# An MLP with fast matrix multiplication: the sums of one weight tile made two periods later, and its store put behind those of six other tiles

## The chip, the cores and the metric

One core of a Trainium2 chip. The metric is the device time of one execution in microseconds (us). "PE" is the tensor engine, "VectorE" (DVE), "ScalarE" (ACT) and "GpSimd" (POOL) are the other engines, and "SP" is the sync engine, which here only issues DMAs.

## The reference, cut to what matters

```python
# x: 16 x 512 x 768, w1: 768 x 3072, b1: 3072, w2: 3072 x 768, all float32
y = np.matmul(x, w1) + b1
y = 0.5 * y * (1.0 + erf(y / np.sqrt(2.0)))          # GELU
return np.matmul(y, w2).astype(np.float32)
```

## The kernel before

Both products use a scheme with seven instead of eight block products (p1 to p7). It needs sums of blocks: of x (`x_sums`), and of each tile of W1 (`prep_wt`: four VectorE subtractions of 128x384). W1 has 12 tiles; a finished tile, with its sums, is also stored to a scratch tensor in HBM (`keep`), from which the later stages load it. In the early stage, which the change touches, the kernel works on two blocks of x ("0" and "1") in a hand-written order of units. Unit (0, k) or (1, k) is W1 tile k with x block 0 or 1.

```python
seq = ([(0, k) for k in range(7)] +
       [(1, 0), (1, 1), (1, 2), (0, 7), (1, 3), (0, 8), (1, 4), (0, 9), (1, 6), ...])
at = {u: n for n, u in enumerate(seq)}          # at[1, 0] == 7, at[1, 1] == 8

def prep_wt(n):                                 # four sums, put in a list; run when sums() pops them
    o = {s: w1_op(wts[n], s) for s in range(7)}
    for d, a, b in ((T3, B22, T1), (T1, T1, B11), (T2, B22, T1), (T4, B21, T2)):
        later(KQ * P, lambda d=d, a=a, b=b: tt(o[d], o[a], o[b], SUB), soon)

def keep(n):
    nc.sync.dma_start(out=w1s[hi_of(n)][:], in_=wts[n])
```

A period works on the new unit i and finishes the previous unit j. Each `fill(slot)` is a place where VectorE sums and DMA issues are put between the parts. bX, bY, bZ and bW are the buffers that PE's products go to, "arena" is the kernel's working memory on the chip, and c22 and c12 are two blocks of the result, each finished by one VectorE add:

```python
p1(i); copy_xy(i)        # PE -> bX;  ScalarE copies bX to bY
p7(j)                    # PE -> bY;  VectorE: c22 add (reads bY)         L608 (in add_c22)
fill(1)
p5(i)                    # PE -> bW;  ScalarE copy
fill(2)
p3(j)                    # PE -> bZ;  VectorE: c12 add                    L636
fill(3)
p6(i)                    # PE -> bY;  VectorE: copy bZ<-bY (even units)   L654
j.right_done()           # ScalarE: GELU, needs both adds of j            L399
fill(4)
p4(j); fill(5)           # PE accumulates into bY of j; ScalarE: GELU     L404
p2(i); fill(6)           # PE -> bX;  ScalarE: GELU                       L404
```

And the part of the early stage's `fill` that is changed (`loads_a` issues the loads of x and of W1 tiles; tile 7 goes into tile 0's buffer, tile 8 into tile 1's):

```python
def fill_a(pos, slot):
    # ... cut ...
    if slot == (1 if pos < at[1, 0] else 4) and pos + 1 < len(seq) and seq[pos + 1][0] == 0:
        prep_wt(seq[pos + 1][1])                # the next unit's tile
    if slot == 4:
        if pos in (3, 4):
            prep_wt(pos - 3)                    # tiles 0 and 1, wanted only from pos 7 and 8 on
    # ... cut ...
    if slot == 1:
        if pos in (at[1, 0] - 2, at[1, 0] - 1): # pos 5 and 6
            h = pos - at[1, 0] + 2
            x_sums(1, soon, slice(h * RH // 2, (h + 1) * RH // 2))
    # ... cut: sums() pops some of the list in slots 1, 2, 4 and 5 ...
    if slot == 5:
        loads_a(pos)
        if pos < 5:
            transposes_a(pos)                   # DMA transposes of x block 1, on SP
        if seq[pos][0] == 1:
            keep(seq[pos][1])                   # stores in the order 0, 1, 2, 3, 4, 6, 5, ...
    if slot == 6:
        flush(soon)
```

## Time and profile before

| | before |
|---|---|
| median of the first 3 runs | 854.24 us (853.19 to 854.71) |
| span of the profile | 852.4 us |
| PE, VectorE, ScalarE busy | 99%, 78%, 49% |
| PE clock | full |

The first line of the profile's page that matters gives the busy time of each engine:

```profile
PE 845.8 (99%) x6432; PEld 569.2 (67%) x6432; DVE 667.8 (78%) x1128; ACT 421.1 (49%) x686; POOL 83.3 (10%) x135
```

A change in the early stage can only win by closing a gap on PE. The timeline of PE in the kernel before, around the place of the change (start, duration, engine, line, operation, then in brackets the idle time before it and what ended it), shows one:

```profile
40.59 0.81 PE L383 MATMUL bZ<-arena 128*128 128x512 f16 x3
41.78 1.46 PE L383 MATMUL bY<-arena 128*128 128x512 f16 x6 [0.38 <-ACT bY L601]
43.08 1.46 PE L383 MATMUL bX<-arena 128*128 128x512 f16 x6
44.39 0.81 PE L383 MATMUL bY<-arena 128*128 128x512 f16 x3
...
46.40 1.46 PE L383 MATMUL bY<-arena 128*128 128x512 f16 x6
47.70 1.46 PE L383 MATMUL bX<-arena 128*128 128x512 f16 x6
```

Read starts, not durations: three matmuls at 40.59 should be followed at 41.24, and the next start at 41.78, so 0.54 us are lost (the bracket says 0.38, because it counts from a modelled end). The six bY matmuls at 46.40 are p6 of one unit and p4 of the unit before it; the bX group follows 1.30 us later, so nothing is lost there.

The chain of waits of the kernel before, over the same stretch, says what the gap at 41.78 hangs on:

```profile
24.64 11.81 DMA arena<-in_w_dram
...
36.47 0.37 DVE arena L189
...
37.61 0.61 DVE arena L636
...
38.24 1.15 ACT arena L399
...
41.13 0.61 ACT bY L601
...
41.78 1.46 PE bY L383 x6
```

W1 tile 6 lands at 36.44 us. Three of its sums come next on VectorE, the c12 add stands behind them, ScalarE's GELU waits for that add, and the copy bY<-bX, which PE needs, stands behind the GELU.

The timeline of VectorE in the kernel before shows the place from which tile 1's sums are taken (four of the five at 33.76) and the place to which they go (behind the last two x sums at 44.24, ahead of the c22 add at 45.30):

```profile
33.76 1.79 DVE L189 TENSOR_TENSOR arena<-arena 128x384 f16<-128x384 f16 x5
35.47 0.68 DVE L608 TENSOR_TENSOR arena<-bY,arena 128x512 f32<-128x512 f32 x1
36.47 1.14 DVE L189 TENSOR_TENSOR arena<-arena 128x384 f16<-128x384 f16 x3 [0.32 <-DMA arena<-in_w_dram]
...
44.24 1.02 DVE L189 TENSOR_TENSOR arena<-arena 128x768 f16<-128x768 f16 x2
45.30 0.69 DVE L608 TENSOR_TENSOR arena<-bY,arena 128x512 f32<-128x512 f32 x1
```

### The profile page before, as it was taken

The page shows a single profiled execution, that of the slowest core. Times are in us where ns is not written, and L with a number is a line of the kernel's source. Part 1 is how long each engine was busy: PE and PEld are TensorE (multiplying, and loading weights), DVE is VectorE, ACT ScalarE, POOL GpSimd, SP SyncE. Part 2 cuts the span into 40 slices and gives each one's busy share as a digit, 9 for nine tenths or more (in the row PEclk, how much of TensorE's full clock was granted, in tenths as well). Part 3 has the DMA queues.
Part 4 walks back from the last instruction along what each step waited for, and adds up shares of the span by engine and source line. Part 5 has one row for each costly group of instructions (what it writes and reads, how often), then busy time and mean ns, then how long its engine had stood idle before and what let it go on. Part 6 is the DMA issues. An engine that isn't in the chain of part 4 may idle for free.

```text
span 852.4 us, 16481 instructions
## 1 busy us (share of the span) xinstructions
PE 845.8 (99%) x6432; PEld 569.2 (67%) x6432; DVE 667.8 (78%) x1128; ACT 421.1 (49%) x686; POOL 83.3 (10%) x135
## 2 busy tenths in 40 slices
PE   9999999999999999999999999999999999999998
PEld 5444445687544897448974499645995469944798
DVE  4956678786657998679976799667996689956998
ACT  4777762122277513774138722477216771267611
POOL 5021100002100002000020000200012000010000
PEclk9999999999999999999999999999999999999999
DMA  9995987649989698996989789896998969967398
GB/s 225 201 271 86 256 166 257 253 190 221 227 242 290 206 326 289 294 265 228 337 285 298 220 279 335 278 300 192 312 343 257 311 177 329 354 218 270 99 310 284
DMA packets 143522, 219.05 MB, mean 257 GB/s; under 512 B 61756, under 2 KB 84724, under 8 KB 143444
## 3 DMA queue, kind: packets, MB, share of 16 engines
q1 hardware_dynamic: 117968, 179.83, 66.0%
q0 software_dynamic: 25440, 38.15, 20.9%
q8 instruction: 50, 0.82, 0.4%
q14 instruction: 28, 0.23, 0.1%
q10 hardware_dynamic: 36, 0.01, 0.0%
HBM read 180.30 MB, written 47.87 MB: 268 GB/s over the span
## 4 chain that ended last, share of the span: by engine, by line
PE 93%; DMA 5%; ACT 1%; DVE 0%; issue 0%; POOL 0%; ACTq 0%
PE bY L383 20%; PE bY L488 15%; PE bX L383 13%; PE bX L488 10%; PE bZ L383 7%; PE bW L383 7%; PE bZ L488 5%; PE bW L488 5%; PE bY L427 5%; DMA arena<-in_x_dram 3%; PE bZ L427 2%; PE bW L427 2%; PE bX L427 2%; DMA arena<-in_w_dram 1%; DMA arena<-w1s 1%; PE bY L575 1%
## 5 line engine op out<-in xcount | busy, mean ns | idle before, releaser
L189 DVE TENSOR_TENSOR arena<-arena 128x1536 f16<-128x1536 f16 (+7 forms) x632 | 403.5, 669 | 6.0 <-PE bW L427 1.1
L383 PEld LDWEIGHTS <-arena 128*128 128x128 f16 x1974 | 192.4, 98 | 225.7 <-DMA arena<-w1s 1.8
L488 PEld LDWEIGHTS <-arena 128*128 128x128 f16 x3528 | 292.1, 98 | 8.4 <-issue 0.4
L383 PE MATMUL bY<-arena 128*128 128x512 f16 x846 | 214.4, 379 | 0.4 <-ACT bY L601 0.4
L608 DVE TENSOR_TENSOR arena<-bY,arena 128x512 f32<-128x512 f32 (+1 forms) x102 | 69.4, 681 | 126.7 <-PE bY L383 88.2
L383 PE MATMUL bX<-arena 128*128 128x512 f16 x564 | 138.6, 379 | 0.6 <-DMA arena<-w1s 0.5
L488 PE MATMUL bY<-arena 128*128 128x192 f16 x1500 | 138.3, 246 | 0.0
L601 ACT COPY bY<-bX 128x512 f32<-128x512 f32 (+1 forms) x143 | 78.6, 550 | 119.4 <-DVE arena L537 82.0
L399 ACT ACTIVATE arena<-arena,b1t 128x1024 f16<-128x1024 f32 x94 | 108.0, 1149 | 54.0 <-DVE arena L636 54.0
L621 ACT COPY arena<-bW 128x512 f32<-128x512 f32 (+1 forms) x147 | 81.0, 551 | 92.0 <-PE bW L488 43.9
L488 PE MATMUL bX<-arena 128*128 128x192 f16 x1020 | 93.1, 246 | 0.1
L636 DVE TENSOR_TENSOR arena<-bZ,arena 128x512 f32<-128x512 f32 (+1 forms) x102 | 69.3, 679 | 22.7 <-PE bZ L383 18.7
L383 PE MATMUL bZ<-arena 128*128 128x512 f16 x282 | 76.2, 379 | 0.0
L383 PE MATMUL bW<-arena 128*128 128x512 f16 x282 | 76.2, 379 | 0.0
L427 PEld LDWEIGHTS <-arena 128*128 128x128 f16 x528 | 51.6, 98 | 34.1 <-issue 0.2
L404 ACT ACTIVATE arena<-bX,b1t 128x512 f16<-128x512 f32 x94 | 64.0, 681 | 10.0 <-PE bX L383 10.0
L520 POOL DMA_DIRECT2D out_dram<-arena x42 | 30.5, 728 | 391.8 <-DVE arena L632 355.6
L404 ACT ACTIVATE arena<-bY,b1t 128x512 f16<-128x512 f32 x94 | 63.3, 674 | 0.0
L652 ACT COPY bZ<-bY 128x512 f32<-128x512 f32 (+1 forms) x54 | 29.0, 537 | 66.0 <-DVE arena L636 31.8
L294 POOL DMA_DIRECT2D arena<-in_x_dram x60 | 32.3, 544 | 265.0 <-DMA arena<-arena 154.6
L488 PE MATMUL bZ<-arena 128*128 128x192 f16 x504 | 48.5, 246 | 0.0
L488 PE MATMUL bW<-arena 128*128 128x192 f16 x504 | 48.5, 246 | 0.0
(60 smaller groups left out, 401.2 us busy)
## 6 DMA issues: line engine op xcount, KB each, us to landing
arena<-w2s SPq DMA_DIRECT2D x294, 288.0 KB, 4.6
arena<-w1s SPq DMA_DIRECT2D x72, 672.0 KB, 6.5
out_dram<-arena POOLq DMA_DIRECT2D x42, 384.0 KB, 4.7
w2s<-arena SPq DMA_DIRECT2D x49, 288.0 KB, 3.9
arena<-in_x_dram POOLq DMA_DIRECT2D x60, 192.0 KB, 6.8
w1s<-arena SPq DMA_DIRECT2D x12, 672.0 KB, 7.8
arena<-in_w_dram POOLq DMA_DIRECT2D x17, 384.0 KB, 7.2
out_dram<-arena SPq DMA_DIRECT2D x17, 384.0 KB, 3.5
```

Source lines behind the costliest of these rows:

```text
L189: nc.vector.tensor_tensor(out=o, in0=a, in1=b, op=op)
L294: nc.gpsimd.dma_start(out=xhs[t], in_=xr[:, sb * 8 + t, :])
L383: nc.tensor.matmul(out=dst[:, 0:RH], lhsT=w1_op(self.wt, slot)[:, c, :], rhs=a[:, c, :], start=first and c == 0, stop=c == self.C - 1, ski ...
L399: nc.scalar.activation(out=self.G[1][:, hi, :, :], in_=self.tmp, func=GELU, bias=b1t[:, 2 * hi + 1:2 * hi + 2])
L404: nc.scalar.activation(out=self.G[0][:, hi, row, :], in_=bank[:, 0:RH], func=GELU, bias=b1t[:, 2 * hi:2 * hi + 1])
L427: nc.tensor.matmul(out=dst[:, 0:N2], lhsT=a, rhs=w[:, :, c, :], start=first and c == 0, stop=c == self.C - 1, skip_group_check=True)
L488: nc.tensor.matmul(out=dst[:, t * N4:(t + 1) * N4], lhsT=a, rhs=w[:, c, :], start=first and c == 0 and t == ts[0], stop=c == NQ - 1, skip_ ...
L520: eng.dma_start(out=orr[:, s0:s0 + 2, right * N2:(right + 1) * N2], in_=self.dst[:, r].rearrange("p t h n -> p t (h n)"))
L601: nc.scalar.copy(out=bY[u.g % 2][:, 0:u.F], in_=bX[u.g % 2][:, 0:u.F])
L608: nc.vector.tensor_tensor(out=u.c22(), in0=bY[u.g % 2][:, 0:u.F], in1=w[:, 0:u.F], op=ADD)
L621: nc.scalar.copy(out=w[:, 0:u.F], in_=bW[:, 0:u.F])
L636: nc.vector.tensor_tensor(out=u.c12(), in0=bZ[:, 0:u.F], in1=w[:, 0:u.F], op=ADD)
```

## The change

Its intent, as the code shows it: tile 1's sums are wanted only from the ninth unit on, so they leave a period in which VectorE is full. Since they are now the last of the first seven tiles' sums, the tile's store becomes the last of the seven stores too, so that the stores go out in the order in which the sums are made.

```diff
             if slot == 4:
-                if pos in (3, 4):
-                    prep_wt(pos - 3)
+                if pos in (3, 6):
+                    prep_wt(pos // 6)
@@
-                if seq[pos][0] == 1:
-                    keep(seq[pos][1])
+                for n in {at[1, 0]: (0, 2, 3, 4, 6, 5), at[1, 1]: (1,)}.get(
+                        pos, seq[pos][1:] if pos > at[1, 6] and seq[pos][0] and seq[pos][1] > 6 else ()):
+                    keep(n)
```

## The prediction

> **What bounds the kernel.** TensorE: the summary of engines has PE busy 845.8 of 852.4 us, VectorE 78%, ScalarE 49%; the granted clock is full. The Trainium skill (Perfetto Trace Analysis, Identifying the Most-Contended Engine) calls matmul busy time a poor measure of closeness to roofline (weight loads are busy 67% here); I use it only to find gaps: the PE timeline is back to back from 20 us on but for 0.38 us at 41.4 and 0.55 us at 376. So the change can win at most about 0.4 us in its stage.
>
> **The period.** In this stage a W1 tile takes 4.53 us of PE: p1 and p2 (bX), p7 (bY), p5 (bW), p3 (bZ), p6 and p4 (bY). VectorE has per period the c22 add (0.69), c12 add (0.69), copy bZ<-bY (0.70), and sums between; four W1 sums take 1.44 to 1.53 us.
>
> **What moves.** The instruction order shows exactly four VectorE sums of 128x384 (W1 tile 1) moved from between the copy at 33.15 us and the c22 add at 35.47, to between the last x sums (44.24 to 45.26) and the c22 add at 45.30. The store of tile 1 (672 KB) goes from second to seventh on the SP queue. No work is added.
>
> **Old place.** The c22 add can start near 34.95 instead of 35.47. That doesn't propagate: the next sums, of tile 6, start at 36.47 because their tile lands only then (the timeline shows 0.32 us of idle, ended by the W1 DMA; the chain of waits runs through that DMA, the three sums, the c12 add, GELU, the copy bY<-bX at 41.13, and PE at 41.78). The 0.38 us gap stays.
>
> **New place.** The c22 add of tile 6 (45.30 to 45.99 before) now begins near 46.70 and ends near 47.4. The matmuls p4 of that tile accumulate into the same bY bank, and the order shows them waiting for VectorE; they began at 47.05. So PE should stall about 0.4 us (0.3 to 0.6). The c12 add, copy and GELU then run some 0.8 us late, but the next uses (bZ at 50.29, bY at 50.93) have over 1 us of slack, and the next period has no sums. PE is back to back afterwards and later loads are released by PE, so the 0.4 us is not given back.
>
> **Stores.** SP issues stores about every 1.2 us from 38.19 to 45.7. After: six tiles from 38.2, ending 1.2 us earlier; tile 1 near 46.8, landing by about 54. Tile 8's load into the same buffer starts at 55.93, released by PE; the store should just not delay it, and tile 8's sums at 66.13 leave 3 us.
>
> **Time.** 854.24 + 0.4 = 854.6 us (runs before: 853.19 to 854.71). 8 in 10: 853.4 to 855.9. Faster by over 2%: 0.003; within 2%: 0.99; slower: 0.007.
>
> **Right or wrong in the profile.** A new PE gap of 0.3 to 0.6 us near 47, ended by the c22 add; the gap at 41.4 kept at 0.3 to 0.5, with tile 6's sums still waiting for their DMA; the c22 add near 35 about 0.5 us earlier; tile 8's load still released by PE near 56; everything after 60 us shifted by 0.4 us.
>
> **What would make it wrong.** Tile 6 landing earlier in other runs (the old place would then gain up to 0.4 us); tile 8 held by the late store, stalling VectorE and PE near 66; run-to-run variation larger than the effect.

## More of the kernel before

PE start times can be compared exactly between traces, because a matmul of 128x512 starts every 0.216 us when nothing holds it: three of them take 0.65 us.

## The result, and the profile after

| | before | after |
|---|---|---|
| median of 6 runs | 854.43 us (853.19 to 855.5) | 854.1 us (853.4 to 855.96) |
| span of the profile | 852.4 us | 854.2 us |

The ratio of after to before is 0.9999, with a 95% interval of 0.9986 to 1.0012. Ratios here are the mean time of one kernel's runs over that of the other's runs of the same rounds, so they are not quite the ratios of the medians. The interval is 2.2 us wide; the predicted 0.4 us is far inside it. The time alone says "same" and nothing about the mechanism, so the traces have to.

The timeline of PE in the kernel after, over the same units:

```profile
40.41 0.81 PE L383 MATMUL bZ<-arena 128*128 128x512 f16 x3
41.84 1.46 PE L383 MATMUL bY<-arena 128*128 128x512 f16 x6 [0.62 <-ACT bY L601]
43.13 1.46 PE L383 MATMUL bX<-arena 128*128 128x512 f16 x6
44.79 0.81 PE L383 MATMUL bY<-arena 128*128 128x512 f16 x3 [0.20 <-DVE bZ L654]
...
46.80 1.76 PE L383 MATMUL bY<-arena 128*128 128x512 f16 x6
48.41 1.46 PE L383 MATMUL bX<-arena 128*128 128x512 f16 x6
```

The group at 46.80 is the predicted place. The next group starts 1.61 us later instead of 1.30: the new stall is 0.31 us. It carries no bracket, because the merged line covers p6 and p4 and the wait is between them; its duration of 1.76 instead of 1.46 shows it too. But there are two further differences: 0.78 us lost at 41.84 (0.54 before), and 0.36 us lost at 44.79 (0.01 before). By start times, PE is 0.18 us ahead of before at 40.41, then loses 0.24 more at 41.84, 0.35 at 44.79 and 0.31 in the group at 46.80, so it is 0.71 us behind at 48.41. (It had been 0.36 us ahead until 39.1, where it lost 0.18 us behind the copy bZ<-bY that follows tile 6's sums and the c12 add.)

The timeline of VectorE in the kernel after:

```profile
34.65 0.69 DVE L608 TENSOR_TENSOR arena<-bY,arena 128x512 f32<-128x512 f32 x1 [0.91 <-PE bY L383]
36.52 1.14 DVE L189 TENSOR_TENSOR arena<-arena 128x384 f16<-128x384 f16 x3 [1.18 <-DMA arena<-in_w_dram]
...
39.59 2.09 DVE L189 TENSOR_TENSOR arena<-arena 128x768 f16<-128x768 f16 x4 [0.26 <-DMA arena<-arena]
...
44.64 2.46 DVE L189 TENSOR_TENSOR arena<-arena 128x768 f16<-128x768 f16 x6
47.02 0.68 DVE L608 TENSOR_TENSOR arena<-bY,arena 128x512 f32<-128x512 f32 x1
```

At the old place the c22 add starts as soon as its matmuls end (34.65), and then VectorE stands idle for 1.18 us until tile 6 lands: the room that was made is spent waiting for a DMA. At the new place the six sums at 44.64 (two of x, four of tile 1) push the c22 add to 47.02.

The chain of waits of the kernel after leads through the x sums, which waited for a DMA transpose of x, then the copy bZ<-bY (which the matmuls at 44.79 need), the moved sums and the c22 add into p4:

```profile
32.28 7.22 DMA arena<-arena
...
44.04 0.70 DVE bZ L654
...
47.02 0.69 DVE arena L608
...
47.76 0.81 PE bY L383 x3
```

That transpose landed at 39.49 here and at 38.84 in the profile of before. Nothing that the change moves comes before 33 us, so this may be a difference between runs and not between kernels. The experiments had to separate the two.

The theory, then: (a) the moved sums cost PE 0.3 us at the new place; (b) they give nothing at the old place, because tile 6's landing alone sets the gap near 41.5 (the runs bear this out only where tile 6 lands late, see below); (c) the reorder of the stores is needed once the sums are late. Rivals: the store order itself changes contention; VectorE is overfull near 41.5, so that relief there pays; PE has slack later that swallows the stall.

### The profile page after: what moved, and what is told of

Read it like the earlier page. It is cut to its first block, busy times and chain, and to the rows that moved or that the text cites. A ratio compares the mean times of both kernels' runs of the same rounds, so it can differ in the third digit from the quotient of the medians.

```text
span 854.2 us, 16480 instructions
## 1 busy us (share of the span) xinstructions
PE 846.5 (99%) x6432; PEld 568.6 (67%) x6432; DVE 667.0 (78%) x1128; ACT 421.2 (49%) x686; POOL 83.4 (10%) x135
## 4 chain that ended last, share of the span: by engine, by line
PE 92%; DMA 5%; DVE 1%; SPq 1%; ACT 0%; issue 0%; POOL 0%; DVEq 0%; ACTq 0%
PE bY L383 19%; PE bY L488 15%; PE bX L383 13%; PE bX L488 10%; PE bW L383 6%; PE bZ L383 6%; PE bZ L488 5%; PE bW L488 5%; PE bY L427 5%; DMA arena<-w1s 3%; PE bZ L427 2%; PE bX L427 2%; PE bW L427 2%; DMA arena<-in_x_dram 1%; PE bY L575 1%; DMA arena<-arena 1%
```

## The experiments

Eleven runs of nine kernels were made; all gave the right result.

### The two kernels again

No edit.

> The kernel before once more. Theory: no stretch at p4(6) near 47 us (p6 and p4 back to back, 1.30 us), the c22 add of tile 6 starts as soon as p7 ends; a gap of 0.3 to 0.7 us near 41.5 as in both first profiles. Landing times of the x transposes (38.2 in the first profile of before, 39.5 in that of after) vary between 38 and 40 with no regard to the version; the sum of waits for w1s varies between 0.5 and 1.5 us. Rival (the transposes land later because of the change): here they land at 38.2 again, and at 39.5 in the repeated after.

> The changed kernel once more, to tell the change from run-to-run variation. Theory (the four moved sums make PE wait for the c22 add of tile 6): the start-to-start step from p6(7) to p4(6)'s following bX group in the period near 47 us is again stretched by 0.3 to 0.5 us against the 1.30 us of an undisturbed pair. Rival (the gap near 44.8 and the later w1s gaps of the first profile come from the change too): they are there again, 0.2 us or more near 44.8 and about 1.3 us of waits for w1s. If instead they come from when the x transposes and W1 loads happened to land, they differ from the first profile while the stretch near 47 stays.

Measured: 854.37 us for before and 856.74 us for after, beside 853.66 us for another run of before. The timeline of PE in the repeat of after:

```profile
40.64 0.81 PE L383 MATMUL bZ<-arena 128*128 128x512 f16 x3
41.34 1.46 PE L383 MATMUL bY<-arena 128*128 128x512 f16 x6
42.64 1.46 PE L383 MATMUL bX<-arena 128*128 128x512 f16 x6
43.94 0.81 PE L383 MATMUL bY<-arena 128*128 128x512 f16 x3
...
45.96 0.81 PE L383 MATMUL bY<-arena 128*128 128x512 f16 x3
46.92 0.81 PE L383 MATMUL bY<-arena 128*128 128x512 f16 x3 [0.15 <-DVE arena L608]
```

The stall between p6 and p4 is there again, 46.92 - 45.96 - 0.65 = 0.31 us, and now its wait is named: the c22 add. The loss near 44.8 is gone; the transpose landed at 37.62 in this run. The gap near 41.4 is 0.05 us. The repeat of before has no stall at p4 (46.46 to 47.75) and 0.59 us at 41.85. So the stall at p4 belongs to the change, and the loss near 44.8 to the run. The expectation that before keeps a gap at 41.5 held; that after might have none stood in the expectation of neither run. The expectation names 38.2 for the transpose in the first profile of before; the trace has 38.84 for its last part, and the repeats have 38.91 (before) and 37.62 (after), so the version does not set it.

The late part varies far more than all this. Against the first profile of before, the last matmul of the repeat of after ends up 2.61 us late, though it was 0.13 us early at 47 us. The waits of PE for W1 tiles that come back from the scratch tensor sum to 3.2 us there, to 1.3 us in the first profile of after, and to 0.5 and 0.8 us in the two of before.

### The store order alone

```diff
-                if seq[pos][0] == 1:
-                    keep(seq[pos][1])
+                for n in {at[1, 0]: (0, 2, 3, 4, 6, 5), at[1, 1]: (1,)}.get(
+                        pos, ...): keep(n)
```

> Store order of after, sums of tile 1 in the old place. Theory (sums alone make the stretch; store order is neutral when the sums are early): no stretch at p4(6), stores of the first seven tiles issued back to back in about 7.5 us from 38 to 39, tile 8's load released by PE near 56. Rival (the order of stores itself changes contention and the DVE or DMA times): gaps near 44.8 to 47 as in the profile of after.

Measured: 857.06 us (one run). No stall at p4: groups at 46.26 and 47.55, 1.29 us apart; no loss near 44.8; the gap near 41.5 is 0.23 us. The stores were issued from 37.89 to 45.75. GpSimd issued tile 8's load at 55.78, and PE did not wait for it. The order of stores alone does nothing in this stage; the high time came from 3.4 us of late waits for scratch tiles, a size that after showed too and before did not in its two profiles. With one profile of this kernel, whether that is more than chance stays open. Over all thirteen traces these waits sum to 0.5, 0.8, 1.5 and 1.6 us in the kernels with the old store order and to between 0 and 3.4 us in those with the new one, so the two are not told apart.

### The late sums alone

```diff
-                if pos in (3, 4):
-                    prep_wt(pos - 3)
+                if pos in (3, 6):
+                    prep_wt(pos // 6)
```

> Sums in the new place, store order of before (tile 1 second). Theory: stretch of 0.3 to 0.5 us at p4(6) as in after; SP, which takes its queue in order, stands at tile 1's store from about 39.5 until its sums end near 46.8, and the stores of tiles 2, 3, 4, 6, 5 follow at about 1.2 us each, up to about 53 to 54; so the store reorder is what keeps six stores from being held for some 7 us. Those late stores share the DMA engines with the loads of tiles 7 and 8 (issued near 52 and 56), whose landing grows from about 5 us to 7 or more, with no PE gap since tile 7 is needed only near 61. Rival (store order does nothing): stores issued at the same times as in after.

Measured: 861.74 us (one run) beside 853.66. The stall at p4 is there (46.75 to 48.35, 1.60 us: 0.30). SP stood 7.4 us at tile 1's store, and issued it and five other stores from 47.08 to 51.48 (starts). So far as expected. But I had put the first use of tile 7 at 61 us, and PE wanted it at 58.06. The timeline of PE:

```profile
57.41 0.81 PE L383 MATMUL bX<-arena 128*128 128x512 f16 x3
62.09 0.82 PE L383 MATMUL bX<-arena 128*128 128x512 f16 x3 [3.87 <-DMA arena<-in_w_dram]
```

Tile 7's load was issued at 52.05, as in after (52.10), but took 10.0 us to land instead of 4.9: it shared the DMA engines with the six stores, the last of which landed at 60.22. The Trainium skill (DMA: Bandwidth & Descriptors, Issuing engines are not separate DMA queues) says that DMAs from different engines run on the same 16 DMA engines and interleave. The trace agrees only in part: the DMA view of 52 to 57 us has 413 packets, all of the queue of SP's stores (queue 1) and none of that of GpSimd's loads (queue 0); the load's first packet started at 57.44, 5.4 us after its issue (1.5 us in after), and the two mixed only from there on. PE lost 4.03 us at once and then 1.7 us more, because its clock fell. The windows view of sums_only (stretch, its length, busy time and count of each engine, granted clock, DMA share, GB/s):

```profile
63.00:64.00 1.00, 1.00 (x4) 0.43 (x3) 0.57 (x2) 0.57 (x1) 0.00 (x0) 0.50 1.38 197
...
66.00:67.00 1.00, 1.00 (x5) 0.45 (x4) 0.42 (x1) 0.00 (x0) 0.16 (x1) 0.84 1.02 184
```

So the store order, which does nothing by itself in this stage, is worth 5.7 us of PE time in this trace once the sums are late (one run; none of the eight other traces with late sums, all with the reorder, has this wait). Given the late sums, the reorder is the part of the change that mattered most.

### More of the suspected cost

Four, then eight, further sums behind the moved ones. They repeat the last one, so the result stays right.

```diff
                 if pos in (3, 6):
                     prep_wt(pos // 6)
+                if pos == 6:
+                    o = {s: w1_op(wts[1], s) for s in (B21, T2, T4)}
+                    for k in range(4):          # 8 in the kernel named triple
+                        later(KQ * P, lambda: tt(o[T4], o[B21], o[T2], SUB), soon)
```

> After, with four more sums (idempotent repeats of T4 of tile 1, result still right) behind the moved ones: the suspected cost twice. Theory (every us that VectorE spends there beyond about 1.0 us of slack goes straight to PE): the stretch at p4(6) grows from 0.3 to 0.5 us by 1.3 to 1.5 us, to about 1.8 us, and the time is 1.2 to 1.6 us above that of after, ratio to before about 1.0020. Rival (PE has slack later that takes it up, or the sums overlap): stretch under 1 us, time within 0.5 us of before.

> After, with eight more idempotent sums behind the moved ones, a larger dose than double, so that the time can show it. Theory (VectorE time there goes one to one to PE, 0.39 us per sum, and is not given back): the step from p6(7) to p4(6), 0.65 us undisturbed, is stretched by 0.31 + 3.1 = 3.4 us (it was 0.31 in both profiles of after and 1.87 with four more sums); time about 3.1 us above after, ratio to before about 1.004. If the idle stretch on PE is long enough to lower the granted clock, as the gap of 3.9 us in sums_only did (granted 0.50 for some 3 us), up to 1.7 us more. Rival (slack later takes it up): ratio to before under 1.0015.

The timeline of PE with four more sums, then with eight more:

```profile
46.01 0.81 PE L383 MATMUL bY<-arena 128*128 128x512 f16 x3
48.53 0.81 PE L383 MATMUL bY<-arena 128*128 128x512 f16 x3 [1.72 <-DVE arena L608]
```

```profile
46.10 0.81 PE L383 MATMUL bY<-arena 128*128 128x512 f16 x3
50.20 1.44 PE L383 MATMUL bY<-arena 128*128 128x512 f16 x3 [3.30 <-DVE arena L608]
```

The stall is 1.87 and 3.45 us (48.53 - 46.01 - 0.65, and likewise). With 0.31 us for none more, each sum costs 0.39 us of PE time, one to one. Times: 856.81 us with four more, ratio to before 1.0015 (0.9992 to 1.0038), which proves nothing by itself; 859.09 us with eight more, ratio 1.005 (1.0038 to 1.0062), some 4.3 us. With eight, the idle stretch also halved the clock (granted 0.50 from 50 to 55 us in the windows view), which cost 2.7 us in its trace and not the 1.7 I had allowed. The profiled run is the slowest of its six, with a mean granted clock of 0.996; the fastest, 857.79 us, has 1.000, so not every run paid this. Of the 5.9 us by which PE is behind just after that, 5.6 us are left at its last matmul. A stall of this size is mostly not given back; in the trace with four more sums, 0.7 us of 1.48 were absorbed at 376 us, where before itself waits for a scratch tile. Whether the 0.3 us of the change itself survive that place, these runs do not show.

### Tile 1's sums one period later still

```diff
-                if pos in (3, 6):
-                    prep_wt(pos // 6)
+                if pos in (3, 7):
+                    prep_wt(pos // 7)
```

> After, with tile 1's sums one period later still (behind the copy bZ<-bY near 48 us, where VectorE stood idle 1.5 to 1.9 us in both versions). Theory: the stretch at p4(6) near 47 is gone (under 0.1 us), no new gap near 50 since T1 of tile 1 is ready near 49 and first used by p5 near 49.6 to 50; time 0.3 to 0.4 us below after and equal to before, ratio 0.999 to 1.001. Rival (T1 comes too late for p5, or c22 add is delayed): PE gap near 50 of 0.2 to 0.8 us.

Measured: 853.84 us, ratio to before 0.9987 (0.997 to 1.0004), so not told apart. The stall at p4 is gone: groups at 47.00 and 48.30, and none follows near 50. The timeline of VectorE shows the four sums in a place where it would have waited anyway (it still waits 0.45 us after them):

```profile
48.53 1.53 DVE L189 TENSOR_TENSOR arena<-arena 128x384 f16<-128x384 f16 x4
50.51 0.69 DVE L608 TENSOR_TENSOR arena<-bY,arena 128x512 f32<-128x512 f32 x1 [0.45 <-PE bY L383]
```

In this run the transpose landed late (39.69) and the loss near 45 was there again, 0.36 us, with the stall gone: the two are separate. (PE also lost 0.42 us at 39.32, behind the same copy as in after at 39.1; tile 6 landed late, at 36.70.)

### Tile 6's sums behind the c12 add

To remove the wait for tile 6 from the chain without removing the wait itself, its sums are put behind the c12 add and the copy of their period; two x sums move to the next period. So the edit takes the wait out of the chain, and the work of three sums with it.

```diff
-            if slot == (1 if pos < at[1, 0] else 4) and ...
+            if slot == (1 if pos < at[1, 0] and pos != 5 else 4) and ...
                 prep_wt(seq[pos + 1][1])
@@  x_sums of pos 5 put in the list at slot 4 instead of 1, then:
             if slot == 6:
-                flush(soon)
+                while len(soon) > (2 if pos == 5 else 0):
+                    soon.pop(0)[1]()
```

> Before (tile 1 in its old place), with tile 6's sums put behind the c12 add and the copy of their period, so that the wait for tile 6's DMA doesn't hold the c12 add. Theory (the 0.4 to 0.6 us gap near 41.5 is the chain tile 6 DMA, its sums, c12 add, GELU, copy bY<-bX): c12 add starts near 36.6 instead of 37.5, the copy bY<-bX ends before 40.9, PE gap at 41.5 under 0.1 us; time 0.4 us lower, ratio to before about 0.9995. Rival (the gap is due to VectorE being overfull in these two periods, as the change supposes): the gap stays or only moves to the next period.

> Both: tile 6's sums behind the c12 add, and tile 1's sums at the period near 48. Theory: no gap at 41.5, none at 47; same as t6_old within 0.2 us, since taking tile 1's sums out of the old place gives nothing even when the DMA wait is gone; ratio to before about 0.9995. Rival (relief at the old place pays once tile 6's wait is out of the way): PE gaps of 0.2 us or more in t6_old between 40 and 47 that are absent here.

> The version without gaps in this stage, again. Theory: no step stretched by more than 0.1 us between 21 and 60 us whatever the landing times; time 0.5 to 1.0 us below after in the mean, ratio to before about 0.9993, within the noise. Rival (the gaps only move): gaps of 0.2 us or more between 21 and 220 us.

Measured: with tile 1 in its old place (t6_old) 854.36 us, ratio 0.9992 (0.9975 to 1.0009); with tile 1 one period later still 854.06 us, ratio 0.9992 (0.9975 to 1.0009), and in the repeat 854.87 us, ratio 0.9999 (0.9985 to 1.0013). In none of the three traces does a PE start come more than 0.06 us late from 21 to 220 us. The timelines of VectorE and PE in t6_old, where tile 1's sums still stand at the old place (the five at 33.57):

```profile
33.57 1.79 DVE L189 TENSOR_TENSOR arena<-arena 128x384 f16<-128x384 f16 x5
35.28 0.68 DVE L608 TENSOR_TENSOR arena<-bY,arena 128x512 f32<-128x512 f32 x1
36.38 0.69 DVE L636 TENSOR_TENSOR arena<-bZ,arena 128x512 f32<-128x512 f32 x1 [0.41 <-PE bZ L383]
...
37.78 2.59 DVE L189 TENSOR_TENSOR arena<-arena 128x384 f16<-128x384 f16 x6
```

```profile
40.40 0.81 PE L383 MATMUL bZ<-arena 128*128 128x512 f16 x3
41.05 1.46 PE L383 MATMUL bY<-arena 128*128 128x512 f16 x6
```

The c12 add now waits only for PE, and the gap at 41 is gone, with the sums of tile 1 untouched. So what made the gap was that sums which wait for a DMA stood ahead of the c12 add. The Trainium skill (PSUM — Partial Sum Buffer, Engine vs sequencer instructions) calls the queues of ScalarE and VectorE strict FIFO, and this is what the trace of after shows: the matmuls of the c12 add had ended at 36.18 (a modelled end), yet VectorE stood idle until tile 6 landed at 36.50, made its three sums, and began the add only at 37.59.

All traces together settle point (b). If tile 6's landing alone sets the gap, the loss at p6 near 41.5 must follow from when tile 6 lands, relative to where PE is. I take PE's place from the bZ group just before:

| trace | tile 1's sums | tile 6 lands | bZ starts | lands - starts + 4.69 | lost at p6 |
|---|---|---|---|---|---|
| before | old | 36.44 | 40.59 | 0.54 | 0.54 |
| before again | old | 36.50 | 40.61 | 0.58 | 0.59 |
| store order alone | old | 36.30 | 40.76 | 0.23 | 0.23 |
| after | new | 36.50 | 40.41 | 0.78 | 0.78 |
| after again | new | 36.00 | 40.64 | 0.05 | 0.05 |
| after, timed | new | 36.07 | 40.52 | 0.24 | 0.24 |
| sums alone | new | 36.79 | 40.71 | 0.77 | 0.78 |
| one period later still | later | 36.70 | 40.61 | 0.78 | 0.78 |
| four more sums | new | 36.04 | 40.72 | 0.01 | 0.02 |
| eight more sums | new | 36.13 | 40.39 | 0.43 | 0.44 |
| tile 6 behind, t6_old | old | 36.30 | 40.40 | 0.59 | 0.00 |

The 4.69 is fitted from the lines; one number fits all ten traces whose tile 6 sums stand ahead of the c12 add, wherever tile 1's sums are. The last line shows the rule broken by the one edit that should break it (the two traces of t6_pos7 break it likewise: 0.00 lost, with 36.36 and 36.29).

But the rule has a floor that (b) left out. With tile 1's sums at the old place, tile 6's sums cannot start before the c22 add lets them. VectorE in store_only shows this limit almost reached, with no wait for the DMA worth a bracket:

```profile
35.64 0.68 DVE L608 TENSOR_TENSOR arena<-bY,arena 128x512 f32<-128x512 f32 x1
36.32 1.14 DVE L189 TENSOR_TENSOR arena<-arena 128x384 f16<-128x384 f16 x3
```

Even so PE lost 0.23 us. Elsewhere VectorE starts its next instruction 0.60 us after such an add (41.04 and 41.64 in this trace). By that, an estimate, the sums could have started at 36.07 at the earliest in before, 0.40 us earlier than they did, which leaves about 0.14 us of the 0.54 (0.16 in its repeat). So that much of the gap is VectorE's load and not the landing. The two traces below this floor, 0.05 us (after again) and 0.02 us (four more sums), both have tile 1's sums moved away and an early landing: there the change earned about 0.1 us at the old place, by estimate. No run has such a landing with the sums at the old place.

### After, timed beside its variants

No edit.

> The changed kernel on the same chip and rounds as its variants. Theory: the stretch at p4(6) of 0.3 us again (third profile); ratio to before 1.0003, not to be told from 1 with an interval of about 0.0015. The gap near 41.5 is 0.8 us where the x transposes or tile 6 land late (39.5 and 36.5 in the first profile) and near 0 where they land early (37.6 and 36.0 in the second). Rival (the change is worth more than 1 us either way): ratio outside 0.9985 to 1.0015.

Measured: 854.38 us, ratio to before 1.0000 (0.9988 to 1.0011). The stall at p4 is there a third time (groups at 46.02 and 47.62: 0.30 us). PE waits for scratch tiles sum to 0.5 us in this trace, the least of the three of after, so the large late waits of the repeat of after do not come with the change every time.

## Why the prediction was right

- *The time.* 854.6 us was predicted, 853.4 to 855.9; measured 854.1 us. The range held, and so did "within 2%". The predicted 0.4 us cannot be seen in the time: both timed sets of after have intervals of about 2 us. A change worth nothing would have met the range as well, so that the time came out right says little; the traces have to carry the mechanism.
- *The new stall.* Predicted about 0.4 us (0.3 to 0.6) before p4, ended by the c22 add. Shown: 0.31, 0.31 and 0.30 us in three traces of after, 0.30 in sums_only, none in before, store_only or pos7; 0.39 us more for each further sum. The term was sized slightly too large.
- *The old place.* Predicted that the c22 add starts 0.5 us earlier and nothing follows. Shown: the repeats put it at 35.06 against 35.49, 0.43 us, the time after it is spent waiting for tile 6, and the table above shows the gap following the landing wherever tile 1's sums are, down to the floor of some 0.15 us for the old place. With tile 6's sums behind the c12 add (t6_old against t6_pos7), both are free of gaps: there, relief at the old place buys nothing.
- *The gap near 41.5.* "Kept at 0.3 to 0.5" was too narrow: lost starts were 0.05 to 0.78 us, by when tile 6 landed. The prediction treated one run's landing time as the kernel's. It also listed an early landing as a way to gain 0.4 us from the change; tile 6 did land early (36.00), and the gap vanished, but by the floor above only about 0.1 us of that is owed to the moved sums; the rest would have vanished with the sums at the old place too.
- *"Everything after 60 us shifted by 0.4 us."* The first profile had 0.71 us. Only 0.31 of it was the change; the rest was the transpose's and tile 6's landing, less PE's head start. And "not given back" holds only up to the first wait for a scratch tile (277 or 376 us); there and later, waits that vary from run to run (0 to 3.4 us in all) can take up the shift or add to it.
- *The stores.* Predicted that tile 1's store lands near 54 and that tile 8's load stays released by PE. Shown: it landed at 53.02, and the load was issued at 56.63, after PE. What I did not predict is how much the reorder was worth: without it the same late sums cost 4.03 us of waiting and 1.7 us of lowered clock in the one trace of that kernel.

What stays open: why the x transpose landed at 39.5 and 39.7 in two traces and between 37.6 and 38.9 in the others, what sets the size of the late waits for scratch tiles, and why no packet of tile 7's load started in sums_only until the stores were nearly through. The version with no gap in this stage (t6_pos7) is the cleanest by its traces, but in time it is not told apart from before or after.

## What to carry to other kernels

Work moved out of a full period gains little if the next instruction on that engine waits for a DMA that lands late anyway; look at what stands behind it before looking at how full the engine is, and put sums that wait for a load behind adds that other engines wait for. Where an engine sits beside a saturated PE, check the place that receives the work as closely as the one that loses it: here 1.44 us of sums into 1.1 us of slack (from 45.99, the end of the c22 add in before, to 47.05, the start of p4) came out as 0.3 us of PE time. When work is made later, move every in-order DMA that waits for it later too, or it holds up the transfers behind it and throws them onto somebody else's loads.

## What the Trainium skill lacked or had wrong

- TensorE: Matmul & The Clock Gate (Part 1: The HAM clock gate) has the clock fall to half after an idle window of about 3.4 us, and calls the windows free-running. The lengths agree: by the granted clock of the windows view it was halved for 3.4 us in sums_only (62.9 to 66.3) and for 6.8 us with eight more sums (49.0 to 55.8). That a whole idle window is needed does not agree: with eight more sums the clock fell 2.1 us after PE's last matmul had ended (46.91, modelled), 1.2 us before the next one; in sums_only it fell 0.8 us after PE had started again. An idle stretch of 1.72 us lowered nothing; 3.30 us cost 2.7 us more and 3.87 us cost 1.7 us more, so the shorter one cost more.
- DMA: Bandwidth & Descriptors (Issuing engines are not separate DMA queues) says that such DMAs interleave, but not what it costs or how long one can stand: a W1 tile load of 384 KB from GpSimd took 10.0 us beside the tail of six stores of 672 KB from SP, and 4.9 us without them, and for the first 5.4 us none of its packets started.
- PSUM — Partial Sum Buffer (Engine vs sequencer instructions) names ScalarE, VectorE and GpSimd as strict FIFO. It does not name SP; in the run with the late sums alone, SP stood 7.4 us at one store whose sums were not made, and five others waited behind it.
